# Where the small tiles of a two-layer encoder trunk lie in SBUF

## The chip, the cores and the metric

The kernel runs on one core of one Trainium2 chip. The metric is the device time of one execution in microseconds (us); each shown time is a median over runs. Engines are named as the profile names them: PE is TensorE's matmul, PEld its weight load (the load of the stationary operand), DVE is VectorE, ACT is ScalarE, POOL is GpSimd, SP is SyncE, which here only issues DMAs.

## What is computed

Two layers of an encoder over 512 tokens of 1024 features, float32. Each layer adds a mixer of three attention branches and then a feed-forward block with a convolution; a final norm follows.

```python
for l in range(DEPTH):
    h = rmsnorm(x, norm1_g[l])
    z = h @ w_in                       # 1024 x 6080: q, k, v, latents, gate logits
    y_na, y_mla, y_gqa = ...           # neighbourhood, latent and sliding-window attention
    merged = sum_i sigmoid(gate_i) * (y_i @ w_br_i)
    x = x + merged @ w_out
    h = rmsnorm(x, norm2_g[l])
    u = conv3(h @ w_up) + conv_b       # 1024 -> 5632
    a, g = split(u)
    x = x + (gelu(g) * a) @ w_down     # 2816 -> 1024
return rmsnorm(x, final_g)
```

## The kernel before

Features lie on the 128 partitions and the 512 tokens on the free axis, so one row of a tile of 512 float32 values takes 2048 bytes of its partition. Every float32 operand of a large product is cut into a high and a low part (`hi`, `lo`, type float32r), by ScalarE (L142) and VectorE (L143). A product is then three matmuls for each 128 rows: hi by hi (L156), lo by hi (L157) and hi by lo (L158), all accumulated in one PSUM bank. The moving operand is an activation tile of 512 columns, the stationary one a 128x128 slice of a weight tile. A product over 1024 features is 24 such matmuls.

The names that the profile shows are these. `raw` is a weight tile as it was loaded, `whi` and `wlo` are its parts (three buffers each, so weights are loaded and split ahead of use). `hh` and `hl` are the parts of the normalised features, which the input projections, the gates and the first feed-forward product (`w_up`) read. `ff` (tags `fh` and `fl`) are the parts of the feed-forward's inner features, which only the last product (`w_down`) reads. `mo` is the merged mixer, read by `w_out`; `yah`, `yal`, `ynh`, `ynl` are attention outputs, read by the branch projections; `mg` are latents. In the attention steps `qn`, `qr`, `kn`, `kr`, `gq`, `gk` are queries and keys, `pt` softmax rows, `ph` and `pl` the transposed rows' parts, `vs` the values.

TensorE's order is written out by hand, in `schedule`. The other engines are ordered by a scheduler that simulates the program; attention steps and weight splits have a raised priority there. Semaphores follow from reads and writes of tiles.

**Where tiles lie.** A tile takes its row's bytes, rounded up to 32, in every partition. Pools are laid one behind another: `const` (features, parameters, norm tiles), then `wp` (the weight tiles `raw`, `whi`, `wlo`), then the pools of the stage that runs: `mx` and the attention pools in the mixer, `ff` in the feed-forward. Nearly all tiles are multiples of 512 bytes per row; these are not: the two parameter tiles `par` (237 values, 960 bytes), `warm` and `neghalf` (32 each), `idb` (256), `ms` and `rt` (4 values each, two buffers, 32 each), `hb` (24 values, 96), `nsink` (32) and the `nm` tiles of the three attentions (32 or 64). Each of these shifts all that lies behind it. In `const` the four buffers of `ms` and `rt` (128 bytes) lie behind `hh` and `hl`; `hb` (96 bytes) lies at the front of `mx`; the pool `ff` has no small tile.

The start bytes modulo 512 that follow, for the operands of matmuls:

| tiles | before | after |
|---|---|---|
| `whi`, `wlo` (weight slices) | 448 | 448 |
| `ff` | 448 | 448 |
| `hh`, `hl` | 320 | 448 |
| `yah`, `yal`, `ynh`, `ynl`, `mo`, `mg` | 32 | 448 |
| `kn`; `qn`, `qr`, `kr` | 32; 160 | 448 |
| `gq` (8 tiles of 64 or 256 phase); `gk` | 64, 256; 64 | 448 |
| `vs`, `ph`, `pl` of the sliding-window attention | 64 | 448 |
| `ph`, `pl` of the latent attention | 352 | 448 |
| `idf`, `ones` (identity, ones) | 0 | 448 |
| `idb`, `gmask` (bf16, masks) | 64; 320 | 64; 320 |

(The latent attention's values lie in `ynh` and `ynl`.) The slice of 64 columns that the rotary key's weights are cut into starts at 448 or 192 in both.

Of the kernel before, what the change touches and what calls it, by code (L numbers as in the profile page):

```python
# [10 lines left out]
F32 = mybir.dt.float32  # L11
F32R = mybir.dt.float32r
BF16 = mybir.dt.bfloat16
# [4 lines left out]
P = 128  # L18
L = 2
# [15 lines left out]
NPC = 45 + 192  # L35
# [23 lines left out]
class Trunk:  # L59
    """Features on partitions, the 512 tokens on the free axis. Every float32 operand of a large  # L60
    product is cut into two float32r parts (hi + lo, exactly); hi*hi + hi*lo + lo*hi accumulate in PSUM.
    TensorE runs in the order of the schedule below, which places each attention step at least one
    dense product after the step it depends on."""

    def __init__(self, ctx, tc, d):
        self.tc, self.nc, self.d, self.ctx = tc, tc.nc, d, ctx
        nc = self.nc
        self.const = ctx.enter_context(tc.tile_pool(name="const", bufs=1))
        self.wp = ctx.enter_context(tc.tile_pool(name="wp", bufs=1))
        self.psum = ctx.enter_context(tc.tile_pool(name="psum", bufs=1, space=bass.MemoryType.PSUM))  # L70
        self.groups, self.turn = {}, {}
        c = self.const
        self.x = [c.tile([P, S], F32, name=f"x{k}") for k in range(KD)]
        self.par = [c.tile([P, NPC], F32, name=f"par{l}") for l in range(L)]
        nc.scalar.dma_start(self.par[0], d["par"][0])
        self.idf = c.tile([P, P], F32, name="idf")
        make_identity(nc, self.idf)
        self.ones = c.tile([P, P], F32, name="ones")
        nc.vector.memset(self.ones, 1.0)
        warm = c.tile([P, 1], F32, name="warm")  # L80
        nc.scalar.activation(warm, self.ones[:, 0:1], AF.Exp)
        self.neghalf = c.tile([P, 4], F32, name="neghalf")
        nc.vector.memset(self.neghalf, -0.5)
        self.idb = c.tile([P, P], BF16, name="idb")
        nc.vector.tensor_copy(self.idb, self.idf)
        gmf = c.tile([P, 2 * P], F32, tag="sq1", name="gmf")
        self.specs, self.raws, self.parts, self.used = [], [], [], 0
        self.plans = [self.schedule(l) for l in range(L)]
        for s, W in self.plans:
            self.specs += [w for item in s for w in W.get(item, ())]  # L90
        nc.sync.dma_start(self.x[0], d["xT"][0:P, :])
        self.fetch(1, 0)
        for k in range(1, KD):
            if k in (4, 5):
                self.fetch(k - 2, 0)
            (nc.scalar if k in (1, 3) else nc.sync).dma_start(self.x[k], d["xT"][k * P:(k + 1) * P, :])
        nc.scalar.dma_start(gmf, d["gmask"])
        nc.scalar.dma_start(self.par[1], d["par"][1])
        self.gmask = c.tile([P, 2 * P], BF16, name="gmask")
        nc.vector.tensor_copy(self.gmask, gmf)  # L100

# [1 line left out]
    def banks(self, **groups):  # L103
# [7 lines left out]

# [1 line left out]
    def fetch(self, n_raw, n_split):  # L113
# [23 lines left out]

# [1 line left out]
    def split(self, hi, lo, src, scale=None):  # L139
# [38 lines left out]
    def rs_tokens(self, pool, acc, dim):  # L178
        nc = self.nc
        ps = self.bank("r")  # L180
        for j in range(4):
            nc.tensor.matmul(ps[:, j:j + 1], acc[:, j * P:(j + 1) * P], self.ones[:, 0:1], start=True, stop=True)
        ms = pool.tile([P, 4], F32, tag="ms", name="ms", bufs=2)
        nc.vector.tensor_scalar(ms, ps[:, 0:4], 1.0 / dim, EPS, ALU.mult, ALU.add)
        rt = pool.tile([P, 4], F32, tag="rt", name="rt", bufs=2)
        nc.gpsimd.tensor_tensor(rt, ms, self.neghalf, ALU.pow)
        return rt
# [33 lines left out]
    def group(self, specs, mv, after):  # L221
        """Four products side by side, the first half of the rows of all of them first: the last
        operands are needed late. after[(half, i)] runs behind that piece."""
        self.gbank = [self.bank("g") for _ in range(4)]
        for n, spec in enumerate(specs):
            hf, i = divmod(n, 4)
            self.mm3(self.gbank[i], self.weights(spec), mv[4 * hf:4 * hf + 4], hf == 0, hf == 1)
            if (hf, i) in after:
                after[(hf, i)]()

# [1 line left out]
    def schedule(self, l):  # L232
# [92 lines left out]

# [1 line left out]
    def norm_begin(self):  # L327
# [12 lines left out]
    def norm_hooks(self, evac):  # L340
        """For group(): the sum of squares behind the first half, its spread behind the second product."""
        def sums():
            rt = self.rs_tokens(self.const, self.acc, D)
            self.dg = self.rs_diag(self.const, "sq0", rt, 1.0)

        def spread():
            self.rb = self.const.tile([P, S], F32, tag="rb", name="rb")
            self.rs_spread(self.dg, self.rb)
            evac(0)
            evac(1)  # L350
        return {(0, 3): sums, (1, 1): spread, (1, 2): lambda: evac(2), (1, 3): lambda: evac(3)}

# [1 line left out]
    def do_mla_open(self):  # L354
        self.banks(g=[0, 1, 2, 3], d=[4, 5, 0, 1, 2, 3], r=[6, 7])
        self.mxs, self.mx = self.open("mx")
        self.mps, self.mp = self.open("ml")
        self.mp2 = self.mps.enter_context(self.tc.tile_pool(name=f"mm{self.l}", bufs=1, reuse_waits="tile"))
        self.rc, self.rsn = (self.mp.tile([P, S], F32, tag=t, name="rope", bufs=2) for t in ("knh", "knl"))
        q = self.nc.gpsimd if self.l else self.nc.sync  # L360
        q.dma_start(self.rc, self.d["rope"][:, :S])
        q.dma_start(self.rsn, self.d["rope"][:, S:])
        self.hb = self.mx.tile([P, 24], F32, tag="hb", name="hb")
        self.nc.vector.tensor_scalar(self.hb, self.pr[:, PC_BG:PC_BG + 24], 0.5, None, ALU.mult)
        self.merged, self.z = [None] * KD, {}
        self.qn, self.kn, self.pts, self.pp, self.y = {}, {}, {}, {}, {}
# [95 lines left out]
    def do_ms(self, h, half):  # L462
        nc, mm = self.nc, self.nc.tensor.matmul
        for b in (2 * half, 2 * half + 1):
            bs = slice(b * P, (b + 1) * P)
            s = self.bank("s")
# [4 lines left out]
            mm(s, self.qr[h][:, bs], self.kr[1], start=False, stop=True)  # L471
            nm = self.mp.tile([P, 2], F32, tag="nm", name="nm", bufs=6)
            nc.vector.tensor_reduce(nm[:, 0:1], s, AX.X, ALU.max, negate=True)
# [24 lines left out]

# [1 line left out]
    def do_na_open(self):  # L500
# [13 lines left out]
    def na_table(self, h):  # L514
        """Row (r, c) of the bias of head h: the window of the padded table that starts at (15 - c, 7 - r)."""
        self.tb[h] = self.np.tile([P, 256], F32, tag="tb", name="tb", bufs=4)
        src = self.d["rpb"][self.l, h]
        self.nc.gpsimd.dma_start(self.tb[h], bass.AP(tensor=src.tensor, offset=src.offset + 15 * 8,
                                                     ap=[[47 * 8, 8], [-8, 16], [1, 256]]))
# [56 lines left out]
    def do_ns(self, h):  # L576
# [5 lines left out]
        for bp in range(2):  # L582
            s = self.bank("s")
            for e in range(2):
# [7 lines left out]
                                           ALU.mult, ALU.add)  # L592
            nm = self.np.tile([P, 4], F32, tag="nm", name="nm", bufs=6)
            nc.vector.tensor_reduce(nm[:, 0:2], pt, AX.X, ALU.max, negate=True)
# [36 lines left out]

# [1 line left out]
    def do_gate(self, b, m):  # L633
# [35 lines left out]

# [1 line left out]
    def do_gq_open(self):  # L671
# [4 lines left out]
        gp = self.gp  # L676
# [5 lines left out]
        self.sink = self.pr[:, PC_SINK:PC_SINK + 8]  # L682
        self.nsink = gp.tile([P, 8], F32, tag="nsink", name="nsink")
        nc.vector.tensor_scalar(self.nsink, self.sink, -1.0, None, ALU.mult)
# [30 lines left out]
    def do_gs(self, i, half):  # L715
# [6 lines left out]
        if half == 0:  # L722
            self.gnm = self.gp.tile([P, 12], F32, tag="nm", name="nm", bufs=3)
        nm = self.gnm
# [58 lines left out]

# [1 line left out]
    def do_out(self, m=None):  # L785
# [173 lines left out]
```

## Time and profile before

| | |
|---|---|
| median of 3 runs | 1782.02 us (1781.76 to 1782.59) |
| span of the profiled execution, first to last instruction | 1779.9 us |
| PE busy, matmuls | 1756.5 us, 8068 |
| DVE busy | 1159.3 us (65%) |
| ACT busy | 861.0 us (48%) |
| mean DMA rate | 87 GB/s |

The profiled execution's own time isn't given apart from its span; the median of the runs stands 2.1 us above that span. A group's row gives a line, an engine, an operation, the tiles, the shape and the count, then the busy time and the mean length of one in ns, then the idle time of the engine ahead of it. Rows of matmuls overlap, since a matmul's end is modelled: the time that a matmul takes of TensorE is the distance from its start to the next start, which the first and the last start of a group give.

### The profile page before, as it was taken

The page shows a single profiled execution, that of the slowest core. Times are in us where ns is not written, and L with a number is a line of the kernel's source. Part 1 is how long each engine was busy: PE and PEld are TensorE (multiplying, and loading weights), DVE is VectorE, ACT ScalarE, POOL GpSimd, SP SyncE. Part 2 cuts the span into 40 slices and gives each one's busy share as a digit, 9 for nine tenths or more (in the row PEclk, how much of TensorE's full clock was granted, in tenths as well). Part 3 has the DMA queues.
Part 4 walks back from the last instruction along what each step waited for, and adds up shares of the span by engine and source line. Part 5 has one row for each costly group of instructions (what it writes and reads, how often), then busy time and mean ns, then how long its engine had stood idle before and what let it go on. Part 6 is the DMA issues. An engine that isn't in the chain of part 4 may idle for free.

```text
span 1779.9 us, 21441 instructions
## 1 busy us (share of the span) xinstructions
PE 1756.5 (99%) x8068; PEld 1428.9 (80%) x8068; DVE 1159.3 (65%) x1884; ACT 861.0 (48%) x1497; POOL 30.4 (2%) x87
## 2 busy tenths in 40 slices
PE   8999999999999999999999999999999999999998
PEld 6778888877888888888877788888778888888886
DVE  6867876886457777743357688668855577777232
ACT  5765645664344444423248565466644344444232
POOL 0010000000000000000000100000000000000000
PEclk9999999999999999999999999999999999999999
DMA  5222232222234333323222232322233333333231
GB/s 163 68 77 78 75 95 77 72 66 76 84 94 119 94 94 94 95 90 104 77 81 66 82 86 66 107 79 58 60 89 101 89 107 95 95 95 95 83 101 65
DMA packets 291319, 155.38 MB, mean 87 GB/s; under 512 B 8720, under 2 KB 287376, under 8 KB 291216
## 3 DMA queue, kind: packets, MB, share of 16 engines
q1 hardware_dynamic: 288576, 148.66, 29.0%
q0 software_dynamic: 1920, 4.47, 0.8%
q8 instruction: 63, 1.03, 0.2%
q10 hardware_dynamic: 720, 0.90, 0.2%
q14 instruction: 40, 0.33, 0.1%
HBM read 151.89 MB, written 2.10 MB: 87 GB/s over the span
## 4 chain that ended last, share of the span: by engine, by line
PE 74%; issue 20%; DVE 3%; ACT 2%; DMA 0%; POOLq 0%; POOL 0%; ACTq 0%; DVEq 0%
PE ps_d L156 17%; PE ps_d L157 17%; PE ps_d L158 17%; PE ps_g L157 5%; PE ps_g L156 5%; PE ps_g L158 4%; PE ps_po L621 1%; PE ps_tp L756 1%; PE ps_tp L607 1%; PE ps_tp L484 1%; DVE wlo L143 1%; PE ps_s L728 1%; ACT pt L475 1%; PE ps_s L729 0%; PE ps_s L588 0%
## 5 line engine op out<-in xcount | busy, mean ns | idle before, releaser
L142 ACT CAST whi<-raw 128x1024 fp32r<-128x1024 f32 (+4 forms) x340 | 301.7, 887 | 658.9 <-PE ps_d L157 381.9
L156 PE MATMUL ps_d<-hh,whi 128*128 128x512 f32 (+1 forms) x1344 | 533.4, 397 | 0.0
L158 PE MATMUL ps_d<-hh,wlo 128*128 128x512 f32 (+1 forms) x1344 | 530.4, 395 | 0.0
L157 PE MATMUL ps_d<-hl,whi 128*128 128x512 f32 (+1 forms) x1344 | 530.3, 395 | 0.0
L143 DVE TENSOR_TENSOR wlo<-raw,whi 128x1024 fp32r<-128x1024 f32 (+4 forms) x340 | 346.2, 1019 | 204.6 <-ACT whi L142 196.5
L158 PEld LDWEIGHTS ps_d<-hh,wlo 128*128 128x128 f32 (+1 forms) x1344 | 252.1, 188 | 60.6
L157 PEld LDWEIGHTS ps_d<-hl,whi 128*128 128x128 f32 (+1 forms) x1344 | 252.2, 188 | 58.3
L156 PEld LDWEIGHTS ps_d<-hh,whi 128*128 128x128 f32 (+1 forms) x1344 | 252.3, 188 | 57.8
L156 PE MATMUL ps_g<-ff,whi 128*128 128x512 f32 x352 | 137.0, 389 | 0.0
L158 PE MATMUL ps_g<-ff,wlo 128*128 128x512 f32 x352 | 137.0, 389 | 0.0
L157 PE MATMUL ps_g<-ff,whi 128*128 128x512 f32 x352 | 136.9, 389 | 0.0
L149 DVE TENSOR_TENSOR u<-ps_d,rb 128x512 f32<-128x512 f32 x80 | 55.3, 692 | 78.2 <-PE ps_d L158 78.2
L149 DVE TENSOR_TENSOR gz<-ps_d,rb 128x512 f32<-128x512 f32 x48 | 33.2, 691 | 83.1 <-PE ps_d L158 82.9
L157 PEld LDWEIGHTS ps_g<-ff,whi 128*128 128x128 f32 x352 | 66.1, 188 | 13.9
L158 PEld LDWEIGHTS ps_g<-ff,wlo 128*128 128x128 f32 x352 | 66.1, 188 | 13.7
L156 PEld LDWEIGHTS ps_g<-ff,whi 128*128 128x128 f32 x352 | 66.1, 188 | 13.7
L818 ACT ACTIVATE c<-u,par 128x512 f32<-128x512 f32 x88 | 71.7, 815 | 4.1 <-DVE u L149 2.5
L143 DVE TENSOR_TENSOR pl<-ps_tp,ph 128x512 fp32r<-128x512 f32 x104 | 68.1, 681 | 6.2 <-ACT ph L142 6.1
L820 DVE SCALAR_TENSOR_TENSOR c<-u,par,c 128x511 f32<-128x511 f32 x88 | 66.1, 751 | 2.9
L819 DVE SCALAR_TENSOR_TENSOR c<-u,par,c 128x511 f32<-128x511 f32 x88 | 65.5, 744 | 0.6 <-ACT c L818 0.6
L824 ACT ACTIVATE c<-c 128x512 f32<-128x512 f32 x44 | 27.8, 632 | 77.6 <-DVE c L820 77.6
L156 PE MATMUL ps_g<-hh,whi 128*128 128x512 f32 x128 | 53.8, 420 | 6.3 <-ACT whi L142 6.3
(257 smaller groups left out, 2587.5 us busy)
## 6 DMA issues: line engine op xcount, KB each, us to landing
raw<-in_w_in_dram SPq DMA_DIRECT2D x86, 512.0 KB, 4.0
raw<-in_w_up_dram SPq DMA_DIRECT2D x80, 512.0 KB, 3.7
raw<-in_w_down_dram SPq DMA_DIRECT2D x32, 512.0 KB, 3.5
raw<-in_w_down_dram SPq DMA_DIRECT2D x16, 384.0 KB, 3.0
raw<-in_w_in_dram SPq DMA_DIRECT2D x18, 256.0 KB, 3.0
raw<-in_w_br_mla_dram SPq DMA_DIRECT2D x16, 256.0 KB, 2.6
raw<-in_w_br_na_dram SPq DMA_DIRECT2D x16, 256.0 KB, 2.6
raw<-in_w_br_gqa_dram SPq DMA_DIRECT2D x16, 256.0 KB, 2.6
```

The lines of the kernel that those rows point to most:

```text
L142: nc.scalar.copy(hi, src)
L143: nc.vector.tensor_sub(lo, src, r32(hi))
L149: self.nc.vector.tensor_tensor(out, a, b, ALU.mult)
L156: mm(ps, sh, mh, start=first and k == 0, stop=False)
L157: mm(ps, sh, ml, start=False, stop=False)
L158: mm(ps, sl, mh, start=False, stop=last and k == n - 1)
L475: nc.scalar.activation(pt, s, AF.Exp, bias=nm[:, 0:1], accum_out=nm[:, 1:2])
L484: self.nc.tensor.transpose(tp[:, b * P:(b + 1) * P], self.pts[h, b][:, kc * P:(kc + 1) * P], self.idf)
L818: nc.scalar.activation(c, u, AF.Identity, bias=pr[:, PC_CB + fi:PC_CB + fi + 1], scale=cw[:, 1:2])
L819: nc.vector.scalar_tensor_tensor(c[:, 1:], u[:, :S - 1], cw[:, 0:1], c[:, 1:], ALU.mult, ALU.add)
L820: nc.vector.scalar_tensor_tensor(c[:, :S - 1], u[:, 1:], cw[:, 2:3], c[:, :S - 1], ALU.mult, ALU.add)
L824: nc.scalar.activation(c, c, AF.Gelu_apprx_tanh)
```

## The change

A pool `small` is opened ahead of `const`, and all small tiles move there: `par`, `warm`, `neghalf`, `idb`, `gmask`, `ms`, `rt`, `hb`, `nsink` and the `nm` tiles. The pool is open for the whole kernel, so its tiles are not tied to a stage's pool any more. `ms` and `rt`, which each pool had of its own, are now one set of two buffers; the `nm` of the latent and of the neighbourhood attention share six buffers, and that of the sliding-window attention has a tag of its own. Every other tile's row is a multiple of 512 bytes, so all of them have one start byte modulo 512, which is 448, the one that the weights had. No instruction is added or removed, and TensorE's order and the order of DMA issues are the same, instruction for instruction.

```diff
+        self.small = ctx.enter_context(tc.tile_pool(name="small", bufs=1))
         self.const = ctx.enter_context(tc.tile_pool(name="const", bufs=1))
...
-        self.par = [c.tile([P, NPC], F32, name=f"par{l}") for l in range(L)]
+        self.par = [self.small.tile([P, NPC], F32, name=f"par{l}") for l in range(L)]
...
-        self.neghalf = c.tile([P, 4], F32, name="neghalf")
+        self.neghalf = self.small.tile([P, 4], F32, name="neghalf")
...
-        ms = pool.tile([P, 4], F32, tag="ms", name="ms", bufs=2)
+        ms = self.small.tile([P, 4], F32, tag="ms", name="ms", bufs=2)
...
-        rt = pool.tile([P, 4], F32, tag="rt", name="rt", bufs=2)
+        rt = self.small.tile([P, 4], F32, tag="rt", name="rt", bufs=2)
...
-        self.hb = self.mx.tile([P, 24], F32, tag="hb", name="hb")
+        self.hb = self.small.tile([P, 24], F32, tag="hb", name="hb")
...
-            nm = self.mp.tile([P, 2], F32, tag="nm", name="nm", bufs=6)
+            nm = self.small.tile([P, 2], F32, tag="nm", name="nm", bufs=6)
...
-            nm = self.np.tile([P, 4], F32, tag="nm", name="nm", bufs=6)
+            nm = self.small.tile([P, 4], F32, tag="nm", name="nm", bufs=6)
...
-        self.nsink = gp.tile([P, 8], F32, tag="nsink", name="nsink")
+        self.nsink = self.small.tile([P, 8], F32, tag="nsink", name="nsink")
...
-            self.gnm = self.gp.tile([P, 12], F32, tag="nm", name="nm", bufs=3)
+            self.gnm = self.small.tile([P, 12], F32, tag="gnm", name="nm", bufs=3)
```

(`warm`, `idb` and `gmask` move in the same way; comments and docstrings go.)

The scheduler of the other engines moves a few instructions. On VectorE the small `nsink` of both layers and `hb` of the second are made earlier. In both layers, at the end of the latent attention, where the neighbourhood attention's first queries are prepared, ScalarE and VectorE change order. On ScalarE this stands there in the first layer before, from the exponentials (L475) of the last two blocks of head 3, over their scaling (L477), to the copies of the neighbourhood attention's queries (`q`, L214 to L219):

```order
L475 ACTIVATE pt,nm<-ps_s,nm 128x512 x2
L477 ACTIVATE pt<-pt,nm 128x512
L142 CAST yah_1186<-ps_po 128x512
L477 ACTIVATE pt<-pt,nm 128x512
L214 CAST q_1363<-mg_1129 64x512
L214 CAST q_1369<-mg_1129 64x512
L219 CAST q_1364<-q_1363 64x512
L218 CAST q_1364<-q_1363 64x512
L218 CAST q_1370<-q_1369 64x512
L219 CAST q_1370<-q_1369 64x512
L142 CAST whi<-raw 128x1024
```

And now (line numbers are one higher, buffer numbers three):

```order
L215 CAST q_1366<-mg_1132 64x512
L476 ACTIVATE pt,nm<-ps_s,nm 128x512
L215 CAST q_1372<-mg_1132 64x512
L220 CAST q_1367<-q_1366 64x512
L476 ACTIVATE pt,nm<-ps_s,nm 128x512
L143 CAST yah_1189<-ps_po 128x512
L219 CAST q_1367<-q_1366 64x512
L478 ACTIVATE pt<-pt,nm 128x512
L219 CAST q_1373<-q_1372 64x512
L220 CAST q_1373<-q_1372 64x512
L478 ACTIVATE pt<-pt,nm 128x512
L143 CAST whi<-raw 128x1024
```

The six copies of the queries stood behind the last scaling; now they stand between the exponentials and the scalings, and the last scaling is the last of the piece. On VectorE the same place reads before:

```order
L473 TENSOR_REDUCE nm<-ps_s 128x1 x2
L476 RECIPROCAL nm<-nm 128x1 x2
L143 TENSOR_TENSOR yal_1187<-ps_po,yah_1186 128x512
L215 TENSOR_TENSOR q_1363<-mg_1129,q_1363 64x512
L215 TENSOR_TENSOR q_1369<-mg_1129,q_1369 64x512
L149 TENSOR_TENSOR gz<-ps_d,rb 128x512
```

And now:

```order
L474 TENSOR_REDUCE nm<-ps_s 128x1 x2
L216 TENSOR_TENSOR q_1366<-mg_1132,q_1366 64x512
L477 RECIPROCAL nm<-nm 128x1
L216 TENSOR_TENSOR q_1372<-mg_1132,q_1372 64x512
L477 RECIPROCAL nm<-nm 128x1
L144 TENSOR_TENSOR yal_1190<-ps_po,yah_1189 128x512
L150 TENSOR_TENSOR gz<-ps_d,rb 128x512
```

The two subtractions that make the queries' low halves stand ahead of each block's reciprocal instead of behind both.

More of the change, by code (lines that the diff above doesn't have):

```diff
@@ L79, in __init__ @@
         nc.vector.memset(self.ones, 1.0)
-        warm = c.tile([P, 1], F32, name="warm")
+        warm = self.small.tile([P, 1], F32, name="warm")
         nc.scalar.activation(warm, self.ones[:, 0:1], AF.Exp)
-        self.neghalf = c.tile([P, 4], F32, name="neghalf")
+        self.neghalf = self.small.tile([P, 4], F32, name="neghalf")
         nc.vector.memset(self.neghalf, -0.5)
-        self.idb = c.tile([P, P], BF16, name="idb")
+        self.idb = self.small.tile([P, P], BF16, name="idb")
         nc.vector.tensor_copy(self.idb, self.idf)
@@ L98, in __init__ @@
         nc.scalar.dma_start(self.par[1], d["par"][1])
-        self.gmask = c.tile([P, 2 * P], BF16, name="gmask")
+        self.gmask = self.small.tile([P, 2 * P], BF16, name="gmask")
         nc.vector.tensor_copy(self.gmask, gmf)
```

## The prediction

> **What bounds the kernel now.** The page's head comes first, then the view of waits for TensorE's matmuls.
>
> ```profile
> span 1779.9 us, 21441 instructions
> PE 1756.5 (99%) x8068; PEld 1428.9 (80%) x8068; DVE 1159.3 (65%) x1884; ACT 861.0 (48%) x1497; POOL 30.4 (2%) x87
> ```
> ```profile
> PE ps_g L156 <- ACT whi L142: 6.3, 1, 6.3
> PE ps_tp L484 <- ACT pt L477: 4.0, 5, 0.9
> PE ps_e L867 <- DVE o L874: 1.8, 1, 1.8
> PE ps_s L728 <- ACT pt L738: 1.2, 2, 0.6
> PE ps_g L157 <- DVE hl L146: 0.7, 1, 0.7
> PE ps_r L182 <- DVE acc L175: 0.6, 1, 0.6
> PE ps_s L467 <- ACT pt L475: 0.6, 1, 0.6
> ```
>
> TensorE is busy 99% of the span, and the seven largest groups of its waits (us in total, times, longest) come to 15.2 us, 6.3 of them the start. So TensorE's own stream is the bound, and a change that adds and removes no instruction can matter in two ways only: in the time from one matmul's start to the next, and in new waits. The next view is that of line 157 in windows of one stage each. Columns: count, length in ns (min/median/max), start of the first and of the last.
>
> ```profile
> L157 PE MATMUL ps_d<-hl,whi x288: 390/393/404, 559.7 to 759.7; 128*128 128x512 f32 x144
> ...
> L157 PE MATMUL ps_g<-ff,whi x147: 389/389/389, 772.2 to 871.5; 128*128 128x512 f32 x147
> ...
> L157 PE MATMUL ps_g<-mo,whi x30: 394/394/394, 478.3 to 498.6; 128*128 128x512 f32 x30
> ```
>
> In these windows TensorE does nothing but triples (L156, L157, L158), so a matmul's **step** is the distance from first to last start, over the gaps between rows, over 3. First feed-forward product (`hl`): 200.0 / 287 / 3 = 232.3 ns. Last product (`ff`): 99.3 / 146 / 3 = 226.7. `w_out` (`mo`): 20.3 / 29 / 3 = 233.3. Shape, type, weights' tiles and line are the same in all three; what differs is the moving tile. By the table of start bytes, `ff` and the weights both start at 448 modulo 512; `hh` and `hl` are at 320 and `mo` at 32. The `ff` rows have no spread at all (389/389/389), the `hl` rows go from 390 to 404. A row's length is its step and 161 to 162 ns, in all three kinds, so where no window holds one kind alone, a length gives a step.
>
> Does the neighbouring work differ instead? The windows' view says how busy the others are.
>
> ```profile
> 560.00:660.00 100.00, 100.00 (x432) 81.09 (x431) 72.69 (x93) 42.98 (x55) 0.00 (x0) 1.00 0.32 95
> ...
> 772.00:872.00 100.00, 100.00 (x443) 82.79 (x442) 30.43 (x33) 24.61 (x30) 1.14 (x2) 1.00 0.32 95
> ...
> 478.00:520.00 42.00, 42.00 (x181) 33.79 (x180) 23.84 (x34) 17.63 (x26) 0.00 (x0) 1.00 0.34 100
> ```
>
> The columns are length, PE, PEld, DVE, ACT, POOL, granted clock, DMA share and GB/s. Clock (1.00) and DMA rate (95) are equal. VectorE is busier where steps are long (72.69 against 30.43 of 100 us), which would be a rival cause. The following rows, line by line over the whole kernel, speak on it.
>
> ```profile
> L770 PE MATMUL ps_po<-ph,vs x40: 389/389/397, 333.7 to 1302.4; 128*128 128x512 f32 x40
> ...
> L470 PE MATMUL ps_s<-kr,qr x32: 388/392/393, 72.9 to 995.8; 128*128 128x512 f32 x32
> ...
> L471 PE MATMUL ps_s<-kr,qr x32: 392/396/397, 73.1 to 996.1; 128*128 128x512 f32 x32
> ```
>
> L770 stands in the middle of the sliding-window attention, and its operands both start at 64: median 389, as `ff`. So equal starts go with the short step beside busy engines too. L470 and L471 are the witness against: `kr` and `qr` both start at 160, and the medians are 392 and 396.
>
> **The change part by part.** *Steps.* After the change both operands of nearly every matmul of 512 columns start at 448, the pair that the `ff` rows show. The counts come from the groups by line and form (L156 and L158 have the counts of L157, and the page gives `ps_d<-hh` at 1344 for each).
>
> ```profile
> L157 PE MATMUL ps_d<-hl,whi x1344: 387/393/404, 35.5 to 1645.8; 128*128 128x512 f32 x190, 128*64 128x512 f32 x2
> L157 PE MATMUL ps_g<-hl,whi x128: 387/393/795, 6.9 to 1422.7; 128*128 128x512 f32 x128
> ```
> ```profile
> L157 PE MATMUL ps_d<-yal,whi 128*128 128x512 f32 x136 | 54.1, 397 | 0.5 <-DVE yal L143 0.5
> ...
> L157 PE MATMUL ps_g<-mo,whi 128*128 128x512 f32 x64 | 25.4, 396 | 0.0
> L157 PE MATMUL ps_d<-mo,whi 128*128 128x512 f32 x64 | 25.4, 396 | 0.0
> L157 PE MATMUL ps_d<-ynl,whi 128*128 128x512 f32 x64 | 25.3, 396 | 0.0
> ...
> L157 PE MATMUL ps_d<-mg,whi 128*128 128x512 f32 x44 | 17.3, 394 | 0.0
> ...
> L469 PE MATMUL ps_s<-kn,qn 128*128 128x512 f32 x32 | 12.6, 395 | 0.0
> ...
> L156 PE MATMUL ps_po<-ph,ynh 128*128 128x512 f32 x32 | 12.6, 394 | 0.0
> ...
> L157 PE MATMUL ps_d<-wlo,yah 128*128 128x512 f32 x8 | 3.2, 397 | 0.0
> ```
>
> - `hh` and `hl`: 3 x (1344 + 128) = 4416 matmuls, 232.3 - 226.7 = 5.6 ns each: 24.7 us.
> - `mo`: 3 x 128 = 384, 233.3 - 226.7 = 6.6 ns: 2.5 us.
> - `yah`/`yal` and `ynh`/`ynl`: 3 x (136 + 64) = 600, at the same start byte and length as `mo`, so 6.6 ns: 4.0 us.
> - The rest: `mg` 3 x 44, six groups of 8 like the last row, scores 5 x 32, value products 3 x 32, in all 436; their lengths of 394 to 397 are 5 to 8 over 389, and I take 5: 2.2 us.
> - `ff` and the sliding-window values are at the short step already: nothing.
>
> Sum 33.4 us. The cover that could fail is only TensorE's own, since its row is the path.
>
> *Short matmuls.* Transposes (128 columns, `idf` as moving operand) have no pair of equal starts in this trace:
>
> ```profile
> L756 PE MATMUL ps_tp<-idf,pt 128*128 128x128 f32 x160 | 20.9, 274 | 0.3
> ...
> L484 PE MATMUL ps_tp<-idf,pt 128*128 128x128 f32 x128 | 17.8, 275 | 4.0 <-ACT pt L477 4.0
> ...
> L607 PE MATMUL ps_tp<-idf,pt 128*128 128x128 f32 x128 | 16.6, 273 | 0.0
> ```
>
> Their three distances (0 against 256, 352 and 224) give the same length to 2 ns, so I take no change. The bound is the 5.6 ns of a long matmul, either way, on these 416: 2.3 us.
>
> *Waits that take some back.* Where TensorE waits for another engine's chain, a faster stream only arrives earlier. By the rows of waits: up to the wait of L182 at the start 48 matmuls run, 48 x 5.6 ns = 0.3 us; five waits of L484, each behind some 30 matmuls, 0.8 us; four more (L728, L467, L157) at about 0.1, 0.4 us. Together 1.5 us. VectorE, the busiest other engine, is at 73% of the feed-forward window; that work in a 2.4% shorter stage is 75%, so no stage changes its bound.
>
> *The moved rows.* Those at the end of the latent attention delay `pt` of head 3, which transposes read:
>
> ```profile
> 118.77 0.69 ACT L475 ACTIVATE pt<-ps_s,nm 128x512 f32<-128x512 f32 x1 [1.47 <-DVE nm L473]
> ...
> 121.47 0.73 ACT L477 ACTIVATE pt<-pt,nm 128x512 f32<-128x512 f32 x1
> 122.10 1.25 ACT L214 CAST q<-mg 64x512 fp32r<-64x512 f32 x2
> ...
> 125.18 0.62 ACT L219 CAST q<-q 64x512 fp32r<-64x512 f32 x1
> 125.82 1.06 ACT L142 CAST whi<-raw 128x1024 fp32r<-128x1024 f32 x1
> ```
> ```profile
> 125.75 1.03 PE L484 MATMUL ps_tp<-idf,pt 128*128 128x128 f32 x8
> ```
>
> Before, the last scaling ended at 121.47 + 0.73 = 122.2, and TensorE read it at 125.75: 3.5 us of slack. Now ScalarE has the whole piece from 118.77 to 125.80 ahead of that end, less the one copy (0.62) that now runs in the 1.47 us of idle time: about 125.2. That leaves some 0.4 us, as TensorE comes about 0.1 us earlier; the weight split behind it starts when it did. I take no wait. If ScalarE also has to stand for VectorE's subtractions, it is up to 0.7 us a layer, 1.4 us in all. The `nsink` and `hb` on VectorE are 32 columns at most, one instruction of the shortest kind each; the shared buffers of `ms`, `rt` and `nm` are reused only stages after their last reader. Nothing for both, with the 1.4 us above as the bound of all of them together.
>
> The sum: 33.4 - 1.5 = 31.9 us off a span of 1779.9 is 1748.0; the median stands 2.1 us above the span, so **1750.1 us**.
>
> **Rivals.** *Equal starts are not enough* (witness L470 and L471). If the pair at 448 of a `hh` tile behaves as the mean of `kr`'s, 394 - 161.5 = 232.5, nothing is gained on `hh`; if as the better one, 392, the step is 230.5 and the gain 4416 x 1.8 + 1420 x 2.8 ns = 11.9 us, so 1770. For it: these two rows alone. Against: 160 is the only one of the equal pairs that isn't a multiple of 64, and 1056 `ff` matmuls have no spread at 448 itself.
>
> *Start bytes play no part*, and `ff` is faster for another reason: 1782. For it: VectorE's share. Against: L770, and that `mo`, with VectorE at 23.84 of 42 us, has the longest step. [...]
>
> *Slower: one phase for all engines.* VectorE and ScalarE now also read and write at the phase that TensorE reads. If that slowed them, the attention stages are the place:
>
> ```profile
> 110.00:340.00 230.00, 230.00 (x1136) 190.55 (x1135) 168.96 (x288) 131.42 (x257) 9.19 (x33) 1.00 0.29 81
> ```
>
> VectorE could lengthen by 36% there (230 / 168.96) before it is the bound. From there each further 10% costs 17 us in this window and as much in the second layer's. The 33 us are used up at about 46%; at 50% it is 2 x (253 - 230) = 47 us, less 32: 1797. Against it stand two rows of the same subtraction, one on tiles at 448 and one on tiles elsewhere:
>
> ```profile
> L143 DVE TENSOR_TENSOR pl<-ps_tp,ph 128x512 fp32r<-128x512 f32 x104 | 68.1, 681 | 6.2 <-ACT ph L142 6.1
> ...
> L143 DVE TENSOR_TENSOR ff<-c,ff 128x512 fp32r<-128x512 f32 x44 | 30.1, 684 | 0.0
> ```
>
> **How the numbers follow.** My forecast has 0.85: 1750.1, from 1746 (the 2.3 us of the transposes, and the rows of 394 to 397 at 7 instead of 5) to 1757 (all waits doubled, the 1.4 us, and a fifth less per step). The partial case has 0.08, about 1760 to 1780. No change has 0.04, slower 0.03. The range 1746 to 1760 holds the forecast's own and the lower edge of the partial one; more than 0.8 lies in it. About 0.2% (3.6 us) is what a measurement can tell from no change: faster 0.93, same 0.04, slower 0.03.
>
> **What would show it.** `ps_d<-hl` at line 158 of the new kernel should read 389 in nearly all rows, with a step of 226.7 to 227 in the windows of the first feed-forward product; `mo` the same; `ff` and the sliding-window values unchanged; VectorE's and ScalarE's lengths unchanged; waits of L485 a little longer, none new behind the moved rows. I am wrong if `hl` keeps a spread over 390, or if VectorE's rows lengthen.

## The result and the profile after

| | before | after |
|---|---|---|
| median of 4 runs | 1781.89 us | 1753.97 us (1753.19 to 1754.50) |
| ratio, with its 95% interval | | 0.9842 (0.9828 to 0.9856) |
| span of the profiled execution | 1779.9 us | 1751.4 us |

The time fell by 27.9 us, 1.6%; the forecast was 1750.1 us. The page's head of the changed kernel reads:

```profile
span 1751.4 us, 21439 instructions
PE 1725.7 (99%) x8068; PEld 1426.3 (81%) x8068; DVE 1158.7 (66%) x1884; ACT 861.4 (49%) x1497; POOL 30.4 (2%) x87
```

(The count differs from the one before by two, in semaphore instructions alone.) TensorE is the bound as before, with 31 us less of it for the same 8068 matmuls. VectorE and ScalarE are within 0.6 us of what they were. The view of the lo-by-hi line (now L158) in windows of one stage each; columns as before: count, length min/median/max, first and last start.

```profile
L158 PE MATMUL ps_d<-hl,whi x295: 389/389/389, 550.1 to 750.0; 128*128 128x512 f32 x148
...
L158 PE MATMUL ps_g<-ff,whi x147: 389/389/389, 760.2 to 859.5; 128*128 128x512 f32 x147
...
L158 PE MATMUL ps_g<-mo,whi x32: 389/389/389, 470.0 to 491.1; 128*128 128x512 f32 x32
```

The spread of `hl` (390 to 404 before) is gone. The step is 199.9 / 294 / 3 = 226.6 ns for `hl` (232.3 before), 99.3 / 146 / 3 = 226.7 for `ff`, as before, and 21.1 / 31 / 3 = 226.9 for `mo` (233.3). All three stages now run at one step. In the windows' view the others' busy times are within 2 us of what they were in windows of the same length (length, PE, PEld, DVE, ACT, POOL, clock, DMA share, GB/s):

```profile
550.00:650.00 100.00, 100.00 (x443) 82.83 (x442) 74.59 (x94) 44.55 (x57) 0.00 (x0) 1.00 0.33 97
760.00:860.00 100.00, 100.00 (x443) 82.84 (x442) 30.40 (x32) 24.71 (x29) 1.14 (x2) 1.00 0.31 93
```

Both stages get 443 matmuls into 100 us, though VectorE is two and a half times as busy in the first. TensorE's waits:

```profile
PE ps_g L157 <- ACT whi L143: 6.0, 1, 6.0
PE ps_tp L485 <- ACT pt L478: 4.0, 5, 1.0
PE ps_e L868 <- DVE o L875: 1.8, 1, 1.8
PE ps_s L468 <- ACT pt L476: 1.6, 2, 1.2
PE ps_s L729 <- ACT pt L739: 1.4, 2, 0.7
PE ps_g L158 <- DVE hl L147: 1.3, 1, 1.3
PE ps_r L183 <- DVE acc L176: 0.7, 1, 0.7
PE ps_d L157 <- ACT yah L143: 0.5, 2, 0.3
PE ps_tp L757 <- DVE pt L748: 0.5, 2, 0.2
PE ps_d L158 <- DVE yal L144: 0.5, 2, 0.2
```

They come to 18.3 us. The seven groups that the prediction shows grew from 15.2 to 16.8, and the pair of L757 is new in the list.

### The profile page after: what moved, and what is told of

It reads as the page before. It is cut to its first block, busy times and chain, and to the rows that moved or that the text cites. A ratio compares the mean times of both kernels' runs of the same rounds, so it can differ in the third digit from the quotient of the medians.

```text
span 1751.4 us, 21439 instructions
## 1 busy us (share of the span) xinstructions
PE 1725.7 (99%) x8068; PEld 1426.3 (81%) x8068; DVE 1158.7 (66%) x1884; ACT 861.4 (49%) x1497; POOL 30.4 (2%) x87
## 4 chain that ended last, share of the span: by engine, by line
PE 71%; issue 21%; DVE 4%; ACT 3%; DMA 0%; POOLq 0%; POOL 0%; ACTq 0%; DVEq 0%
PE ps_d L157 16%; PE ps_d L159 16%; PE ps_d L158 16%; PE ps_g L158 5%; PE ps_g L157 5%; PE ps_g L159 4%; PE ps_po L622 1%; PE ps_tp L757 1%; PE ps_tp L608 1%; DVE wlo L144 1%; PE ps_tp L485 1%; ACT pt L476 1%; PE ps_s L729 1%; ACT rsw L206 1%; PE ps_s L590 0%
## 5 line engine op out<-in xcount | busy, mean ns | idle before, releaser
L157 PE MATMUL ps_d<-hh,whi 128*128 128x512 f32 (+1 forms) x1344 | 526.9, 392 | 0.0
L159 PE MATMUL ps_d<-hh,wlo 128*128 128x512 f32 (+1 forms) x1344 | 523.4, 389 | 0.0
L158 PE MATMUL ps_d<-hl,whi 128*128 128x512 f32 (+1 forms) x1344 | 523.1, 389 | 0.0
L158 PEld LDWEIGHTS ps_d<-hl,whi 128*128 128x128 f32 (+1 forms) x1344 | 251.7, 187 | 51.5
L158 PE MATMUL ps_g<-ff,whi 128*128 128x512 f32 x352 | 136.9, 389 | 0.0
L158 PEld LDWEIGHTS ps_g<-ff,whi 128*128 128x128 f32 x352 | 66.1, 188 | 13.8
L143 ACT CAST ph<-ps_tp 128x512 fp32r<-128x512 f32 x104 | 57.1, 588 | 6.0 <-PE ps_tp L485 3.0
```

Of the source, the lines that this page charges most:

```text
L143: nc.scalar.copy(hi, src)
L157: mm(ps, sh, mh, start=first and k == 0, stop=False)
L158: mm(ps, sh, ml, start=False, stop=False)
L159: mm(ps, sl, mh, start=False, stop=last and k == n - 1)
```

## The experiments

All are edits of the changed kernel unless said otherwise. Most add unused tiles only, so that instructions and their order stay (but for one memset of each such tile). Line numbers shift by what each edit adds. Each run's own runs of the kernel before lay between 1781.6 and 1782.3 us in the median.

**Does the shared start count, or 448?** (`e1_all0`)

```diff
         self.small = ctx.enter_context(tc.tile_pool(name="small", bufs=1))
+        pad = self.small.tile([P, 16], F32, name="pad0")
+        nc.gpsimd.memset(pad, 0.0)
```

> The changed kernel with 64 bytes more at the front of the pool of small tiles: all operands still start at one byte modulo 512, but at 0 instead of 448. Theory (what counts is that the moving operand and the stationary one start at the same byte): same time as the changed kernel, 1754 us within 3, step of the hl matmuls in the first feed-forward product 226.7 ns. Rival (448 itself, or some alignment of it, is what counts): steps of 230 ns and more, 1770 us or more.

Measured: 1753.0 us, ratio 0.9836 (0.9819 to 0.9852), and in the first feed-forward product:

```profile
L160 PE MATMUL ps_d<-hl,whi x280: 389/389/390, 550.0 to 739.7; 128*128 128x512 f32 x140
```

The theory held: with all operands at 0 the time is that with all at 448 (1753.97 us) to 1.0 us, so at these two the shared byte's value plays no part.

**Start bytes alone, with the pools and the order of before.** (`e2_padded`, an edit of the kernel before)

```diff
+        pad = self.const.tile([P, 96], F32, name="padc")
+        self.nc.gpsimd.memset(pad, 0.0)
...
         self.hb = self.mx.tile([P, 24], F32, tag="hb", name="hb")
+        pad = self.mx.tile([P, 104], F32, name="padm")
+        self.nc.gpsimd.memset(pad, 0.0)
```

> The kernel before, with its pools and its order, and two unused tiles: 384 bytes behind hh and hl in const, 416 bytes beside hb in mx, so that hh, hl, mo, mg, ya and yn start where the weights do (modulo 512). The attention pools keep their small tiles. Theory (start bytes are all of it): 1754 to 1758 us. Rival (the gain is from small tiles that no longer tie stages together, or from the moved rows): 1782 us.

Measured: 1754.12 us, ratio 0.9844 (0.9829 to 0.9859), the changed kernel's to 0.2 us.

```profile
L157 PE MATMUL ps_d<-hl,whi x280: 389/389/390, 550.1 to 739.8; 128*128 128x512 f32 x140
```

So neither the pool nor the moved rows bring anything that can be told from these times; two pads in the old kernel (the first behind `hh` and `hl`) do the whole.

**The pool and the order of after, with the distances of before.** (`e3_undo`)

```diff
         self.const = ctx.enter_context(tc.tile_pool(name="const", bufs=1))
+        self.gap = ctx.enter_context(tc.tile_pool(name="gap", bufs=1))
+        pad = self.gap.tile([P, 32], F32, name="gap0")
+        nc.gpsimd.memset(pad, 0.0)
...
+        pad = self.mx.tile([P, 24], F32, name="padm")
+        self.nc.gpsimd.memset(pad, 0.0)
         self.hb = self.small.tile([P, 24], F32, tag="hb", name="hb")
```

> The changed kernel, with its pool of small tiles, and two unused tiles that bring back the distances of before: 128 bytes between const and the weights, 96 bytes at the front of mx. Theory: 1778 to 1784 us, hl at 232 ns a step. Rival (pools and order): 1754 us.

Measured: 1783.7 us, ratio 1.0009 (1.0000 to 1.0019): all of the gain is gone again.

```profile
L161 PE MATMUL ps_d<-hl,whi x272: 392/396/399, 550.1 to 739.8; 128*128 128x512 f32 x136
```

The step is 189.7 / 271 / 3 = 233.3 ns. If the pool and the moved rows cost something, it is at most about 3 us, and by this interval perhaps nothing.

**One term alone.** (`e4_gap128`: the first pad of `e3_undo` without the second, so `hh` and `hl` alone lie 128 bytes off.)

> The changed kernel with the 128 bytes between const and the weights alone: hh and hl start 128 bytes off the weights, everything else on them. Theory: the term of hh and hl alone comes back, 4416 matmuls of some 5.4 ns, so 1754 + 24 = 1778 us; mo, ya and yn stay at 227 ns. Rival: 1754 us.

Measured: 1777.18 us, ratio 0.9975 (0.9965 to 0.9985), 23.2 us over the changed kernel; the term of `hh` and `hl` was 24.7 us in the prediction. Over the whole run, line lo-by-hi:

```profile
L161 PE MATMUL ps_d<-hl,whi x1344: 387/393/405, 36.3 to 1642.3; 128*128 128x512 f32 x190, 128*64 128x512 f32 x2
L161 PE MATMUL ps_g<-ff,whi x352: 388/389/395, 767.7 to 1762.0; 128*128 128x512 f32 x176
...
L161 PE MATMUL ps_g<-mo,whi x64: 389/389/390, 476.1 to 1372.4; 128*128 128x512 f32 x64
```

`hl` is back at 393, `mo`, which keeps the weights' byte here, stays at 389. So the term of `hh` and `hl` comes back by itself. All the other terms together are the 6.5 us between this run and `e3_undo`; the prediction had 2.5 + 4.0 + 2.2 = 8.7 us for them.

**The modulus.** (`e8_gap256`, `e11_gap64`, `e12_gap192`: the same gap with 64, 16 and 48 values.)

> The changed kernel with 256 unused bytes between const and the weights: hh and hl start 256 bytes off the weights, everything else on them. Modulus 512: about 1778 us, hl at 231 to 233 ns. Modulus 256: 1754 us.

> The changed kernel with 64 unused bytes between const and the weights: all of hh and hl lie 64 bytes off the weights, with nothing else between neighbouring matmuls changed (in the run with eight distances each pair stood alone among others, which may have lengthened it by itself). If 256 is the modulus, as the 256-byte run says: about 1777 us, hl at 231 to 234 ns. If a distance of 64 does as well: 1754 us. A time below 1752 us would be a better distance than none.

> As the run with 64 bytes, with 192: the same two outcomes, 1777 or 1754 us, and a third if the sign of the distance matters (64 and 192 then differ by some us).

Measured, with the row of lo-by-hi in the first feed-forward product of each:

| gap in bytes | median us | ratio (95%) |
|---|---|---|
| 64 | 1778.98 | 0.9982 (0.9971 to 0.9994) |
| 128 | 1777.18 | 0.9975 (0.9965 to 0.9985) |
| 192 | 1764.35 | 0.9900 (0.9872 to 0.9929) |
| 256 | 1754.09 | 0.9841 (0.9812 to 0.9869) |

```profile
L161 PE MATMUL ps_d<-hl,whi x271: 393/393/398, 550.3 to 739.3; 128*128 128x512 f32 x136
```
```profile
L161 PE MATMUL ps_d<-hl,whi x280: 389/389/389, 549.8 to 739.5; 128*128 128x512 f32 x140
```

The first row is that of 64, the second that of 256. Of the two outcomes named for 256 bytes the second came: of the distances tried, **256 does as well as 0 (1754.09 us beside 1753.97) and 64, 128 and 192 do not, so in these runs the modulus is 256, not 512**; the change asks for more than is needed. At 192 bytes the three lines differ:

```profile
L160 PE MATMUL ps_d<-hh,whi x278: 394/394/394, 549.7 to 739.9; 128*128 128x512 f32 x139
...
L161 PE MATMUL ps_d<-hl,whi x277: 388/388/388, 550.0 to 739.5; 128*128 128x512 f32 x139
...
L162 PE MATMUL ps_d<-hh,wlo x277: 392/392/392, 550.2 to 739.7; 128*128 128x512 f32 x139
```

The step is 189.5 / 276 / 3 = 228.9 ns on the mean, and 189.0 / 270 / 3 = 233.3 at 64 bytes, so 64 and 192 bytes are not alike: modulo 256 they are one distance with two signs, and here the sign counts (14.6 us). No distance tried beats 0 and 256.

**Eight distances in one run.** (`e5_curve_a`, `e6_curve_b`)

```diff
+        if k not in self.padded:
+            self.padded.add(k)
+            n = 0 if k == 0 else 16
+            if n:
+                pad = self.const.tile([P, n], F32, tag=f"pad{k}", name="pad")
+                self.nc.gpsimd.memset(pad, 0.0)
         hi = self.const.tile([P, S], F32R, tag=f"hh{k}", name="hh")
```

(and, in the second, a gap of 8 values between `const` and the weights)

> The changed kernel with 64 unused bytes ahead of each next pair hh, hl: the eight pairs start 64, 128, 192, 256, 320, 384, 448 and 0 bytes behind the weights (modulo 512). If 512 is the modulus, only the last pair (distance 0) has a length of 389; with 256, the pair at 256 too; with 128 or 64, those at 128, 256, 384 or all. A distance with a still shorter step than 226.7 ns would show here as well; the theory names none. Time between 1765 and 1785 us by the first, 1754 by the last.

> As the run before, with 32 bytes more between const and the weights: the eight pairs start 32, 96, 160, 224, 288, 352, 416 and 480 bytes behind the weights. By the theory no pair has the short step. Time 1775 to 1785 us.

Measured, one run each: 1773.88 and 1776.75 us. From the starts in the trace, grouped by pair, the three steps of the triples at 0 and at 256 are 226, 236 and 228 ns (medians of 84 to 168 each), those of the six other pairs of the first run 228 to 233, those of the second run 227 to 240. The line's lengths in the feed-forward window show no 389 even for the pairs at 0 and 256:

```profile
L158 PE MATMUL ps_d<-hl,whi x273: 393/394/398, 550.3 to 739.3; 128*128 128x512 f32 x137
```

This is a miss of the design: a pair that lies right among pairs that don't has only part of the gain (690 ns a triple instead of 680), so the run can't give a curve. The gaps above, which move all pairs together, can. Two things can still be read from the medians. In the first run any two pairs that lie 256 bytes apart have the same three steps to 1 ns, which speaks for the modulus of 256. In the second run they don't (231, 227 and 230 ns at 32 bytes, 231, 236 and 234 at 288), so there the distance modulo 256 doesn't fix a pair's steps; whether the pairs ahead of it do isn't shown by this run.

**Which load must agree?** (`e7_wlo128`, `e10_wlo_hl`)

```diff
+            if i == 0:
+                pad = self.wp.tile([P, 32], F32, tag="padw", name="padw")
+                nc.gpsimd.memset(pad, 0.0)
             lo = self.wp.tile([P, 1024], F32R, tag="wlo", name="wlo", bufs=WB)
+            if i == 0:
+                pad = self.wp.tile([P, 96], F32, tag="padv", name="padv")
+                nc.gpsimd.memset(pad, 0.0)
```

> The changed kernel with 128 unused bytes between whi and wlo (and 384 behind wlo), so that of the three matmuls of a triple only those that involve wlo see another start byte. While a matmul streams, the next one's weights are loaded. If the stream is held up by the load that runs beside it, the step of line lo-by-hi (its neighbour loads wlo) is long, 232 ns, and the other two are 227: 2200 long steps, 1754 + 12 = 1766 us. If the matmul's own weights count, the step of hi-by-wlo is long instead, at the same time. If one long step spoils its neighbours, all three are long, 1780 us or more.

Measured: 1779.05 us, ratio 0.9982 (0.9971 to 0.9993). The three lines of a triple in the first feed-forward product:

```profile
L163 PE MATMUL ps_d<-hh,whi x275: 389/389/389, 549.8 to 739.7; 128*128 128x512 f32 x138
...
L164 PE MATMUL ps_d<-hl,whi x275: 396/396/396, 550.0 to 740.0; 128*128 128x512 f32 x138
...
L165 PE MATMUL ps_d<-hh,wlo x274: 397/397/397, 550.2 to 739.5; 128*128 128x512 f32 x137
```

This is none of the three outcomes named. Not one line is long but two: that beside which `wlo` is loaded (396) and that which multiplies with it (397). Each line's length has no spread at all, though VectorE and ScalarE are busy in this stretch (in the same window of `e3_undo` for 73%, 138.38 of 190 us, and for 44%, 83.54), so their accesses are no likely cause. `e10_wlo_hl` was to separate them: `hl` in a pool of its own, 128 bytes off `hh` as `wlo` is off `whi` (on top of the edit of `e7_wlo128`; 128 unused bytes follow `hl`, and the last stage's tiles that share its buffers move with it).

```diff
+        self.hlp = ctx.enter_context(tc.tile_pool(name="hlp", bufs=1))
+        pad = self.hlp.tile([P, 32], F32, name="pada")
+        nc.gpsimd.memset(pad, 0.0)
...
-        lo = self.const.tile([P, S], F32R, tag=f"hl{k}", name="hl")
+        lo = self.hlp.tile([P, S], F32R, tag=f"hl{k}", name="hl")
```

> As the run with wlo moved by 128 bytes, and hl moved by 128 as well (a pool of its own), so that modulo 256 hh lies with whi and hl with wlo, 128 apart from the other two. Beside each streamed matmul of hh and hl, the load that runs next to it now has the stream's byte (hh beside whi, hl beside wlo, hh beside whi), but the matmul's own weights are off in lo-by-hi and in hi-by-wlo. If the load beside the stream is what counts: all three of hh and hl at 227 ns, long steps are left in ff, mo, ya, yn and mg alone, about 1763 us. If the own weights count: two of three long for hh and hl, about 1782 us.

Measured: 1778.05 us, ratio 0.9980 (0.9969 to 0.9992), and the lines in the same window:

```profile
L166 PE MATMUL ps_d<-hh,whi x275: 387/397/398, 549.7 to 739.7; 128*128 128x512 f32 x138
...
L167 PE MATMUL ps_d<-hl,whi x275: 392/399/400, 550.0 to 739.9; 128*128 128x512 f32 x138
...
L168 PE MATMUL ps_d<-hh,wlo x274: 388/392/395, 550.2 to 739.5; 128*128 128x512 f32 x137
```

Agreement with the load beside the stream alone isn't enough: none of the three lines has the constant 389. The time is nearer to that expected for the matmul's own weights, but that reading has hi-by-hi short, and its median is 397. The starts in the same window show why the medians mislead: the triples alternate. One takes 224, 232 and 226 ns, the next 236, 235 and 234, with the same bytes modulo 256 in both (medians of 33 or 34 for each place in a product). In `e4_gap128` single matmuls alternate in the same way, between 229 or 230 and 237 or 238 ns. So a step isn't fixed by the bytes modulo 256 of its own matmul and of the load beside it. That what ran ahead makes the rest is my reading; the runs show that it can count behind a transpose (`e9_dummy`, below: 228 to 234 ns instead of 226 to 227). What the runs do show: where stream, own weights and next weights all have one byte modulo 256, and the neighbouring matmuls the same one, every step of the stage is 226 to 227 ns (the changed kernel from 550 to 750 us, without exception); at every other placement tried some steps were longer. That all of these must agree for one short step is not shown: hi-by-hi in `e7_wlo128` keeps 227 ns beside neighbours that differ. Which of them costs what alone stays open.

**What is left over 226.7 ns.** (`e9_dummy`)

```diff
-            self.conv(fi, self.dense(self.spec(), self.h))
+            st = self.weights(self.spec())
+            ps = self.bank("d")
+            self.nc.tensor.transpose(ps[:, :P], self.ones, self.idf)
+            self.mm3(ps, st, self.h)
+            self.conv(fi, ps)
```

> The changed kernel with one unused 128-column transpose ahead of each product of the first feed-forward stage (80 in all; the product overwrites its result). That stage has no attention work and shows 389/389/389 in the changed kernel. Theory on what is left over 226.7 ns in the attention stages: a matmul of another shape puts the stream out of step, and the next eight or so matmuls are 2 to 5 ns long each before the step is 227 again, 20 to 25 ns a transpose in all, here too. Rival: the rest comes from the busy VectorE and ScalarE of the attention stages; then the steps here are 227 from the second matmul on. Time 1754 + 80 x (109 + 93 for the first matmul + 22) ns = 1772 us by the first, 1770 by the second; the steps decide.

Measured: 1766.16 us, ratio 0.9913 (0.9884 to 0.9941). The timeline behind one of the added transposes (start, length, engine, line, operation):

```profile
604.60 0.27 PE L813 MATMUL ps_d<-idf,ones 128*128 128x128 f32 x1
604.62 0.48 PE L157 MATMUL ps_d<-hh,whi 128*128 128x512 f32 x1
604.94 0.40 PE L158 MATMUL ps_d<-hl,whi 128*128 128x512 f32 x1
605.17 0.39 PE L159 MATMUL ps_d<-hh,wlo 128*128 128x512 f32 x1
605.40 0.40 PE L157 MATMUL ps_d<-hh,whi 128*128 128x512 f32 x1
```

Over 36 such places, the distances from start to start behind the transpose are 315, 232, 231, 234, 228, 228, 231, 228, 229, 229 ns (means), and from the eleventh on 226 to 227. The second to the tenth are together 30 ns over 226.7. The theory held, in a stage without attention work; that it explains all that is left in the attention stages is not shown. The size was off: the transpose itself takes 26 ns of the stream, not 109, so one costs 26 + 88 + 30 and a few ns ahead of the next, 0.15 us, 80 of them 12 us: 1754 + 12 = 1766.

## Why the prediction was right, and where it was off

*The bound and the cause.* Right: steps follow the start bytes. `e2_padded` has them without the pool (1754.12 us), `e3_undo` the pool without them (1783.7 us), and the gain goes with the bytes both times. The rival that start bytes play no part falls. The rival that equal starts are not enough falls as a forecast, but not as a mechanism: where the neighbours differ, equal starts need not be enough (392 and 396 ns in `e2_padded`, below; 690 ns a triple in `e5_curve_a`). The prediction had neither that nor that 256 bytes do as well as none (`e8_gap256`, 1754.09 us); both did no harm because the change gives all operands one byte.

*The witness against* (`kr`, `qr` at 392 and 396 with equal starts) is answered: those products stood between others (`kn` at 32, `qn` at 160) that differed. `e2_padded` tells this apart from the byte 160 itself. By the sizes of its pads `kr` and `qr` both lie at 448 there, but `kn` at 320, and the lengths are those of before:

```profile
L474 PE MATMUL ps_s<-kr,qr x32: 388/392/397, 71.4 to 980.9; 128*128 128x512 f32 x32
L475 PE MATMUL ps_s<-kr,qr x32: 392/396/398, 71.6 to 981.1; 128*128 128x512 f32 x32
```

In the changed kernel, where all share a byte, the rows read

```profile
L471 PE MATMUL ps_s<-kr,qr x32: 389/389/397, 71.5 to 980.7; 128*128 128x512 f32 x32
...
L472 PE MATMUL ps_s<-kr,qr x32: 387/389/398, 71.7 to 980.9; 128*128 128x512 f32 x32
```

and `e5_curve_a` shows the same for single pairs of `hh` and `hl` (690 ns a triple instead of 680). My reading that 160 fails as no multiple of 64 was wrong: 448 is one.

*The terms.* 33.4 us of steps were forecast. The groups by line and form give the lengths after (the first three lines are hi-by-hi, hi-by-lo, lo-by-hi of `hh` and `hl`):

```profile
L157 PE MATMUL ps_d<-hh,whi 128*128 128x512 f32 x1328 | 520.5, 392 | 0.0
L159 PE MATMUL ps_d<-hh,wlo 128*128 128x512 f32 x1328 | 517.2, 389 | 0.0
L158 PE MATMUL ps_d<-hl,whi 128*128 128x512 f32 x1328 | 516.8, 389 | 0.0
...
L157 PE MATMUL ps_d<-yah,whi 128*128 128x512 f32 x136 | 54.2, 399 | 0.5 <-ACT yah L143 0.5
...
L158 PE MATMUL ps_d<-yal,whi 128*128 128x512 f32 x136 | 53.2, 391 | 0.5 <-DVE yal L144 0.5
L159 PE MATMUL ps_d<-yah,wlo 128*128 128x512 f32 x136 | 53.1, 391 | 0.0
```

Before, the means of `hh` and `hl` were 397, 395 and 395: 5, 6 and 6 ns less, 5.7 on the mean against the 5.6 forecast. `yah` and `yal` went from 403, 397 and 395 to 399, 391 and 391: 4.7 ns instead of the 6.6 that I took from `mo`. That is the term that was mis-sized, and with it the last of the four: these products stand among transposes and short matmuls, and behind a transpose nine steps are long in `e9_dummy` (228 to 234 ns), which would account for it. With 4.7 on 600 matmuls the term is 2.8 us, not 4.0. The starts in the two traces give every term (the time from each matmul's start to the next one's, waits left out): `hh` and `hl` 24.2 us against 24.7, `mo` 2.6 against 2.5, `yah` to `ynl` 3.1 against 4.0, the other 436 matmuls 1.6 against 2.2, `ff` and the sliding-window values 0.3 against nothing.

*Short matmuls.* Right that transposes gain nothing themselves: L485, L608 and L757 stand at 276, 272 and 275 ns (275, 273 and 274 before). They lose a little: from start to next start the 160 of L757 take 110.8 ns on the mean instead of 106.2, and all transposes together 0.9 us, which is within the bound of 2.3 us given for them. With that the steps come to 30.8 us instead of 33.4, as TensorE's busy time says (1756.5 to 1725.7).

*Waits that take some back.* Right in kind and too small. The seven groups grew by 1.6 us, as the 1.5 forecast, but that is luck: the waits of L485, priced at 0.8 us, stand at 4.0 us as before, and those of L468 grew by 1.0 us instead. (They read 1.4 us in `e2_padded`, with the old order, and 0.6 in `e3_undo`, with the new one, so they come with the shorter steps and not with the moved rows.) And the smaller ones that were not in the list grew too (18.3 us in all, against 15.2 and the two of 0.5 and 0.3 that the view of before also has: 2.3 us).

*The moved rows.* Right that no wait comes of them, by less than I gave. In the first layer:

```profile
123.60 0.72 ACT L478 ACTIVATE pt<-pt,nm 128x512 f32<-128x512 f32 x1
```
```profile
124.34 1.04 PE L485 MATMUL ps_tp<-idf,pt 128*128 128x128 f32 x8
```

The scaling ends at 124.32 and TensorE reads it at 124.34. The 3.5 us of slack are used up, instead of leaving 0.4; the place stands on the edge. In the second layer it is the same (the scaling ends at 987.94, TensorE starts at 987.96).

*The slower rival* falls: VectorE's same subtraction is at 682 (`pl`, which moved to 448) and 684 ns (`ff`), 681 and 684 before, and its busy time is 0.6 us less.

*The sum.* Of the 3.9 us between 1750.1 and 1753.97, 2.6 are steps (30.8 us instead of 33.4), 0.8 are waits (2.3 instead of 1.5), and 0.5 is that the median stands 2.6 us over the span this time, not 2.1. The last says nothing of the kernel: the profiled execution itself took 1753.19 us, 1.8 over its span, and is the fastest of the four.

## What to carry to other kernels

When matmuls run back to back, compare the step of groups of the same shape; if a group has a constant length and others spread a few ns above it, look at where their operands start. Here 5 to 7 ns of 232 went away by giving them all one start byte (232.3 and 233.3 became 226.6 and 226.9); a distance of 256 bytes between them did as well as none (1754.09 us beside 1753.97), and two pads of a few hundred bytes in the old kernel were enough (`e2_padded`, 1754.12 us), without touching its instructions. Keep small per-partition tiles out of the pools that hold matmul operands, or pad them; and align all operands of a stage, since one that differs can lengthen its neighbours too (in `e5_curve_a` the pairs at 0 and 256 bytes took 690 ns a triple among others that differed, instead of 680).

## What was not expected of the hardware

- A gap of 256 bytes did as well as none: 1754.09 us beside 1753.97, where gaps of 64, 128 and 192 gave 1778.98, 1777.18 and 1764.35 us.
- A transpose lengthened more than the matmul behind it (`e9_dummy`): after one of 128 columns the first matmul of 512 columns took 315 ns from start to start, and the next nine 228 to 234 before the step was 226 to 227 again.
